# A hybrid decoder step on one core: normed rows held back behind the former pair's factors, two down groups in three token chunks, and the first problem's final rows ordered later

## The chip, the cores and the metric

The kernel runs on one core of a Trainium2 chip. The core has five engines that run on their own and meet through semaphores: TensorE (PE, with its weight loads shown as PEld), VectorE (DVE), ScalarE (ACT), GpSimd (POOL) and SyncE (SP), which here issues nearly all DMAs. The metric is the device time of one launch in microseconds (us). Times of this kernel's runs lie within 1 us of each other.

## The reference

One layer of a decoder for 1024 prompt tokens and 64 sample tokens (8 sequences of 8), 1088 tokens in all, with a model width of 1024:

```python
x += merge_out(attention(h), short_conv(h)) @ w_out          # h = rmsnorm(x) @ w_in, split in 11 parts
h = rmsnorm(x, norm_ffn);  gu = h @ w_gate_up                # 1024 -> 2 x 2816
x = x + (silu(gu[..., :D_FF]) * gu[..., D_FF:]) @ w_down     # 2816 -> 1024
gate = sigmoid(rmsnorm(x, norm_ple) @ w_ple_gate)            # 1024 -> 1024
x = x + (p @ w_ple) * gate                                   # 256 -> 1024
y = rmsnorm(x, norm_final)
```

The change touches the second half only: the norm before gate-up, the down projection, and the final norm's output. All of it is in float32 accuracy.

## The kernel before, in words

**Layout.** Activations are kept transposed: 128 features on the partitions, tokens along the free axis. `x1` holds the running sum as 8 blocks of 128 features by 1088 tokens. Every float32 operand is split into a high and a low part, and a product is three matmuls: high by high, low by high, high by low.

**Two problems.** From the output projection on, the tokens are cut into two problems of 544 (`p` = 0 and 1), and each into two halves of 272 columns (`CW`); a result fits one PSUM bank. There are five banks under the tag `pj` (for these results), two under `at` and one under `po`. The input projection, earlier, cuts the same 1088 tokens into three chunks instead, `CH`: 384, 384 and 320 columns.

**Order of the second half** (`order`, run by `run_rows` and `run_pair`): output projection of both problems; the rows of `w_ple` (`pw_pass`, both problems, copied out of PSUM by ACT in `evac_pw2`, and stored to DRAM); 22 gate-up blocks (`run_pair`, seven products instead of eight for a 2 by 2 block product; the first passes run as block 0 on problem 0, block 1 on problem 0, block 1 on problem 1, block 0 on problem 1); the down projection in four groups of the 22 blocks, `GR`: 4, 6, 6 and 6; then the gate of the last step (`w_ple_gate`) for problem 0 and, in two segments "a" (288 columns) and "b" (256), for problem 1.

**The planner.** The program is written out by a planner, `Weaver`. Every piece of work is a generator; it yields a condition (an event `Ev` with a planned time, or buffers of a ring). `Weaver` keeps a planned clock for each engine, and in each round steps the first side stream that is ready at PE's planned time (and while DVE and ACT are planned at most 5 us ahead of PE), otherwise the main stream of matmuls. What is stepped is written to the engines' instruction queues at once. So the planned times set only the order of instructions on each engine; on the chip an engine executes its queue in that order and waits where it must. `W.later(...)` orders a store or load when its planned time has come.

**The norm before gate-up.** When a problem's last block of `x1` is summed, `rstd` computes the factors and `norm` runs: it broadcasts them over the partitions by two matmuls into the `at` banks, and then, for each of four pairs of feature blocks (`b`, `b` + 4), takes three buffers of 128 by 544 from the ring `Q`, writes four normed half rows on DVE (L139) and spawns `factors`. That stream makes the seven combinations that the seven products need: three differences on DVE (L135), casts of two, two, two and one half rows to high parts on ACT (L131, `lead`), the remainders to low parts on DVE (L135, `rest`), one further difference, and gives its buffers back. `Q` has six buffers in the norm of problem 0 and ten in that of problem 1 (`places`, `room`). A row of `w_ple` needs two of them to begin.

**Down projection.** `down_pass` orders, for each of 8 output blocks `k`, the rows of a group: for each problem and each half one bank of 3 matmuls for each of the group's weight blocks. `evac_down` adds the bank to `x1` on DVE. `down_rows` reads the hidden rows back from DRAM by problem, and `row_in` splits them; `ev_md[g][p]` is the event that the rows of problem `p` are there.

**Final rows.** `fin` works through the token tiles of a segment (five for problem 0, three for "a", two for "b"): 8 transposes on PE (L197) into two banks (`at`, or `pj` for "b"), then `finish`: half a tile scaled on ACT (L131), half on DVE (L144), the banks given back, and the store ordered on SP (L163). For problem 0 and segment "a" `finish` runs after every tile, for "b" after both.

**Lines in the profile.** Helpers record most instructions, so rows carry their lines: L131 ACT, L135 and L139 and L144 DVE, L150 POOL, L154 and L190 and L197 and L186 PE, L163 the DMAs on SP.

Of the kernel before, what the change touches and what calls it, by code (L numbers as in the profile page):

```python
# [17 lines left out]
OP = mybir.AluOpType  # L18
# [8 lines left out]
KT = DM // P  # L27
# [14 lines left out]
CH = [(0, 384), (384, 384), (768, 320)]  # L42
LF = SEQ + 2

CW, PW = 272, 544
# [270 lines left out]
def hybrid_decoder_step(ctx, tc, I, O):  # L316
    nc = tc.nc
    W = Weaver(nc)
# [33 lines left out]
    def psum(tag):  # L352
        W.cur.t = max(W.cur.t, W.take(tag))
        return PS["pool"].tile([P, 512], F32, tag=tag, name=tag, bufs=PS["n"][tag])
# [266 lines left out]
    def free_ps():  # L621
        W.give("pj")
# [393 lines left out]
    g = {}  # L1016
# [604 lines left out]
    N_ = {}  # L1621
# [127 lines left out]
    def cols(ap):  # L1749
        return ap.rearrange("p a b -> p (a b)")  # L1750
# [6 lines left out]
    def room(p):  # L1757

        pool, a = (apool, "A") if p == 0 else (N_["bp"], "B")
        fac[p] = [pool.tile([P, 28, CW], F32, tag=f"{a}_{e}", name=f"f{p}_{e}") for e in ("hi", "lo")]  # L1760
        for e in ("hi", "lo"):
            t = pool.tile([P, 2, PW], F32, tag=f"{a}_{e}x", name=f"q{p}_{e}")
            extra.setdefault(p, []).extend([t[:, 0, :], t[:, 1, :]])
        places(*extra[p])

    def getq(n):
        out = []
        for _ in range(n):
            W.take("Q")
            out.append(Qs.popleft())  # L1770
        return out

    def giveq(*qs):
        for q in qs:
            if any(q is x for x in leaving):
                leaving[:] = [x for x in leaving if x is not q]
                if not leaving:
                    ev_left.t = W.cur.t
                continue
            Qs.append(q)  # L1780
            W.give("Q")
# [13 lines left out]
    def factor(p, i, b):  # L1795
        return [t[:, b * 7 + TI[i], :].bitcast(F32R) for t in fac[p]]

    def factors(p, b, qa, qb, qt, done):

        hi, lo = fac[p]  # L1800
        b11, b12, b21, b22, t1, t2 = (q[:, j * CW:(j + 1) * CW] for q in (qa, qb, qt) for j in range(2))

        def part(t, s, n):
            return cols(t[:, b * 7 + s:b * 7 + s + n, :])

        def lead(q, s, n):
            W.act(part(hi, s, n).bitcast(F32R), q, AF.Copy, n * CW)
            return W.cur.t

        def rest(q, s, n, t, pool):  # L1810
            W.cur.t = t
            (W.pool_tt if pool else W.tt)(part(lo, s, n).bitcast(F32R), q, part(hi, s, n), OP.subtract, n * CW)

        W.tt(t1, b12, b11, OP.subtract, CW)
        W.tt(t2, b22, t1, OP.subtract, CW)
        W.tt(b12, b22, b12, OP.subtract, CW)
        t0 = W.cur.t
        yield None
        tb = lead(qb, 2, 2)
        W.cur.t = t0  # L1820
        yield None
        ta, W.cur.t = lead(qa, 0, 2), t0
        tt = lead(qt, 4, 2)
        W.cur.t = tb
        yield None
        rest(qb, 2, 2, tb, False)
        W.tt(b21, b21, t2, OP.subtract, CW)
        yield None
        tc_ = lead(b21, 6, 1)
        W.cur.t = ta  # L1830
        yield None
        rest(qa, 0, 2, ta, False)
        giveq(qa)
        te, W.cur.t = W.cur.t, tt
        yield None
        rest(qt, 4, 2, tt, False)
        giveq(qt)
        te = max(te, W.cur.t)
        W.cur.t = tc_
        yield None  # L1840
        rest(b21, 6, 1, tc_, False)
        giveq(qb)
        W.cur.t = max(te, W.cur.t)
        done()
# [62 lines left out]
    def norm(p, gfun, ev):  # L1907

        x1 = N_["x1"]
        ns, ev_r = rs.pop(p)  # L1910
        yield ev_r
        if p not in fac:
            room(p)
        yield {"at": 2, "Q": 1}
        (dg,), bc = getq(1), [psum("at"), psum("at")]
        for j, (o, m) in enumerate(TT[p]):
            W.ts(dg[:, o:o + m], ident[:, :m], ns[:, 8 + j:9 + j], None, OP.mult, None, m)
        W.cur.t += 1.5
        yield None
        for h in range(2):  # L1920
            W.mm(bc[h][:, :CW], ones, dg[:, h * CW:(h + 1) * CW], CW, True, True, f32=True)
        giveq(dg)
        left, t0 = [4], W.cur.t

        def done():
            left[0] -= 1
            if left[0] == 0:
                ev.t = W.cur.t - 1.0
        for b in range(4):
            W.cur.t = t0  # L1930
            yield {"Q": 3}
            qa, qb, qt = getq(3)
            for q, k in ((qa, b), (qb, b + 4)):
                for h in range(2):
                    s = slice(h * CW, (h + 1) * CW)
                    W.stt(q[:, s], bc[h][:, :CW], gfun(k), x1[:, k, p * PW + h * CW:p * PW + (h + 1) * CW], OP.mult, OP.mult, CW)
            if b == 3:
                W.give("at", 2)
            W.spawn(factors(p, b, qa, qb, qt, done))

    def norm_rows(p, gfun, ev):

# [40 lines left out]
    def add_square(p, k, n, gfun, evs, last=False, how=None):  # L1983

        n[p] = n.get(p, 0) + 1
        s = square(p, k, n[p] == 1, last)
        if n[p] < KT:
            yield from s
            return
        n[p] = 0  # L1990
        yield from s
        start_rstd(p, 0.0 if p == "b" else 1.0 if gfun is g_ffn else 4.0)
        if gfun is None:
            return
        W.spawn((how or norm)(p, gfun, evs[p]))
# [56 lines left out]
    GR = [(0, 4), (4, 6), (10, 6), (16, 6)]  # L2052
    ev_near = Ev()
    ev_gu, ev_gr = [Ev(), Ev()], [Ev() for _ in GR]
    ev_md = [[Ev(), Ev()] for _ in GR]
    M = {}
# [32 lines left out]
            ev.t = W.cur.t  # L2089

    def evac_down(g, k, p, h, ps):
        xs = N_["x1"][:, k, p * PW + h * CW:p * PW + (h + 1) * CW]
        W.tt(xs, ps[:, :CW], xs, OP.add, CW)
        free_ps()
        if g == len(GR) - 1 and h == 1:
            W.spawn(add_square(p, k, n_down, g_ple, ev_h3, how=norm_rows))

    PLE_H = {0: {0: (0, CW), 1: (CW, CW)}, 1: {"a": SEG["a"], "b": SEG["b"]}}
    pw = {}

# [14 lines left out]
    def evac_ple(k, p, h, ps):  # L2115
        o, n = PLE_H[p][h]
        seg = 0 if p == 0 else h
# [36 lines left out]
    y_s = O["y_sample"].rearrange("b t d -> (b t) d")  # L2154
# [5 lines left out]
    def fin(p):  # L2160
        x1, c0 = N_["x1"], SEG[p][0]
        done = []
        if p == "a":
            y_places()
        yt = N_["bp"].tile([P, 5, DM], F32, tag="B_hi", name="y") if p == 0 else N_["y_ab"][p]

        def finish():
            ns, ev_r = rs[p]
            yield ev_r
            t1 = W.cur.t  # L2170
            for j, (o, m), tag, bk, t_ in done:
                W.cur.t = max(t1, t_)
                yield None
                y = yt[:m, j, :]
                r, tok = ns[:m, 8 + j:9 + j], c0 + o
                t2 = W.cur.t
                W.act(y[:, 0:512], bk[0][:m, :], AF.Copy, 512, scale=r)
                t3, W.cur.t = W.cur.t, t2
                W.ts(y[:, 512:], bk[1][:m, :], r, None, OP.mult, None, 512, fast=False)
                W.cur.t = max(t3, W.cur.t)  # L2180
                W.give(tag, 2)

                def store(tok=tok, m=m, y=y):
                    mp_ = max(0, min(m, SEQ - tok))
                    if mp_:
                        W.store(y_p[tok:tok + mp_], y[:mp_])
                    if mp_ < m:
                        W.store(y_s, y[mp_:])
                W.later(store)
            done.clear()  # L2190
        for j, (o, m) in enumerate(TT[p]):
            tag = "pj" if p == "b" else "at"
            yield {tag: 2}
            bk = [psum(tag), psum(tag)]
            for k in range(KT):
                yield ev_x[p][k]
                W.tr(bk[k // 4][:m, (k % 4) * P:(k % 4 + 1) * P], x1[:, k, c0 + o:c0 + o + m], ident)
            done.append((j, (o, m), tag, bk, W.cur.t))
            if p != "b" or j == 1:
                yield from finish()  # L2200
# [61 lines left out]
    def rows_of(src, k, evac, **kw):  # L2262
        return dict(block(src, k * P, evac, None, **kw), k=k)

    order = []
# [17 lines left out]
    def down_pass(g, ks, ps):  # L2283
        f0, n = GR[g]
        bs = [rows_of(I["w_down"], k, lambda *a: evac_down(g, *a), row0=f0 * P, nk=n) for k in ks]
        order.append(("rows", bs, ps, lambda: M[g], ev_md[g], 0, ev_gr[g] if ks[-1] == KT - 1 else None))

    def ple_pass(p):
        for ks in [(k,) for k in range(KT)] if p == 0 else [(0,), (1,), (2,), (3,), (4,), (5, 6, 7)]:
            order.append(("rows", [rows_of(I["w_ple_gate"], k, evac_ple) for k in ks], (p,), lambda: N_["h3"], ev_h3, 2, None, None,  # L2290
                          PLE_H))

# [183 lines left out]
```

## Time and profile before

| | |
|---|---|
| time, median of 3 runs | 1997.98 us (1997.33 to 1998.3) |
| profiled execution | 1997.44 us, span 1995.7 us |
| PE busy | 1944.2 us (97%) |
| DVE busy | 1277.0 us (64%) |
| POOL busy | 742.7 us (37%) |
| ACT busy | 713.1 us (36%) |
| mean granted PE clock | 0.989 |

Times in a trace count from the span's start. A group or timeline row names the line, the engine, the operation, output and inputs by the program's names (buffer numbers left out), the shapes, and in brackets the idle time of the engine before it and what ended it. A row of PE's waits gives the total, the number and the longest. A row of busy times by window gives the window, its length, busy time (and instructions) of PE, PEld, DVE, ACT and POOL, the granted PE clock as a share of full speed, the share of DMA engines busy, and GB/s. Matmuls are pipelined: the length shown of one is longer than the distance to the next one's start.

### The profile page before, as it was taken

The numbers are of one execution on the slowest core, as the hardware profiler recorded it, in microseconds if no ns is written. First come the engines' busy times: TensorE is split into PE (matmuls) and PEld (weight loads), VectorE is DVE, ScalarE is ACT, GpSimd is POOL, SyncE is SP. The second block draws the span as 40 slices with busy tenths as digits, with TensorE's granted clock in tenths as the row PEclk, the third lists the DMA queues.
The fourth block names the chain that finished last, engine by engine and source line by source line (L and its number), as shares of the span: only waits on it lengthen the run. The fifth ranks groups of instructions, "written<-read, shape, count | busy, mean of one in ns | idle before, by whom it ended". The sixth has DMA issues, their size and how long they took to land.

```text
span 1995.7 us, 36382 instructions
## 1 busy us (share of the span) xinstructions
PE 1944.2 (97%) x13585; PEld 1864.6 (93%) x13585; DVE 1277.0 (64%) x2727; ACT 713.1 (36%) x1448; POOL 742.7 (37%) x661
## 2 busy tenths in 40 slices
PE   8998999999999999999999899999999999999998
PEld 6987879999999999779999899999999999999988
DVE  6635899899988896323438776566666653314754
ACT  5354443312433325433334532232232322213543
POOL 2533445323223242214444233232232354424873
PEclk9999999999999999999999899999999999999999
DMA  4664325222222222446453332222222343212343
GB/s 151 177 192 110 107 83 151 65 56 73 78 73 55 56 64 72 125 118 187 127 157 113 131 95 86 66 81 81 71 79 79 122 151 106 91 43 85 105 152 96
DMA packets 291243, 205.27 MB, mean 103 GB/s; under 512 B 28448, under 2 KB 270680, under 8 KB 291066
## 3 DMA queue, kind: packets, MB, share of 16 engines
q1 hardware_dynamic: 290822, 202.85, 34.1%
q8 instruction: 107, 1.75, 0.4%
q14 instruction: 70, 0.57, 0.1%
q10 hardware_dynamic: 244, 0.09, 0.0%
HBM read 151.43 MB, written 51.31 MB: 102 GB/s over the span
## 4 chain that ended last, share of the span: by engine, by line
PE 81%; DVE 5%; POOL 2%; issue 2%; DMA 1%; ACT 1%; DVEq 0%; SPq 0%; POOLq 0%; ACTq 0%
PE pj L154 42%; PE pj L190 27%; PE at L186 5%; PE po L186 4%; PE pt L197 3%; POOL wl L150 1%; DVE scores L139 1%; DVE ru L135 0%; DMA q_hi<-ple_scr 0%; POOL x L150 0%; DVE junk L1225 0%; DVE x L135 0%; POOL whl L150 0%; DVE q_lo L135 0%; PE at L197 0%
## 5 line engine op out<-in xcount | busy, mean ns | idle before, releaser
L150 POOL TENSOR_TENSOR wl<-wraw,wh 128x512 fp32r<-128x512 f32 (+2 forms) x233 | 298.9, 1286 | 651.1 <-ACT wh L131 642.1
L190 PE MATMUL pj<-h_hi,wh 128*128 128x384 f32 (+2 forms) x1197 | 406.6, 340 | 0.3 <-ACT wh L131 0.3
L190 PE MATMUL pj<-h_hi,wl 128*128 128x384 f32 (+2 forms) x1197 | 393.6, 329 | 0.7 <-POOL wl L150 0.7
L190 PE MATMUL pj<-h_lo,wh 128*128 128x384 f32 (+2 forms) x1197 | 393.3, 329 | 0.0
L131 ACT ACTIVATE wh<-wraw 128x512 fp32r<-128x512 f32 (+2 forms) x233 | 141.5, 610 | 279.7 <-PE pj L154 137.6
L190 PEld LDWEIGHTS pj<-h_hi,wh 128*128 128x128 f32 (+1 forms) x1197 | 225.9, 189 | 16.3 <-issue 12.4
L190 PEld LDWEIGHTS pj<-h_lo,wh 128*128 128x128 f32 (+1 forms) x1197 | 226.1, 189 | 2.5
L190 PEld LDWEIGHTS pj<-h_hi,wl 128*128 128x128 f32 (+1 forms) x1197 | 225.4, 188 | 1.8 <-POOL wl L150 1.1
L154 PE MATMUL pj<-f_hi,whl 128*128 128x272 f32 x1056 | 206.0, 288 | 0.0
L154 PE MATMUL pj<-f_hi,wl 128*128 128x272 f32 x704 | 203.6, 289 | 0.5 <-DVE wl L135 0.5
L154 PE MATMUL pj<-f_hi,wh 128*128 128x272 f32 x704 | 203.3, 289 | 0.0
L154 PE MATMUL pj<-f_lo,wh 128*128 128x272 f32 x704 | 202.6, 288 | 0.0
L154 PE MATMUL pj<-m_hi,wh 128*128 128x272 f32 x644 | 186.2, 289 | 1.0 <-ACT tha L131 0.5
L154 PE MATMUL pj<-m_hi,wl 128*128 128x272 f32 x644 | 185.9, 289 | 0.0
L154 PE MATMUL pj<-m_lo,wh 128*128 128x272 f32 x644 | 185.8, 289 | 0.0
L135 DVE TENSOR_TENSOR x<-pj,x 128x272 f32<-128x272 f32 x160 | 69.5, 437 | 173.6 <-PE pj L154 170.5
L154 PEld LDWEIGHTS pj<-f_hi,whl 128*128 128x128 f32 x1056 | 168.8, 189 | 0.0
L154 PE MATMUL pj<-f_lo,whl 128*128 128x272 f32 x528 | 152.4, 289 | 0.0
L154 PEld LDWEIGHTS pj<-f_hi,wl 128*128 128x128 f32 x704 | 132.9, 189 | 0.7 <-DVE wl L135 0.7
L154 PEld LDWEIGHTS pj<-f_hi,wh 128*128 128x128 f32 x704 | 132.8, 189 | 0.0
L154 PEld LDWEIGHTS pj<-f_lo,wh 128*128 128x128 f32 x704 | 132.7, 189 | 0.0
L154 PEld LDWEIGHTS pj<-m_hi,wh 128*128 128x128 f32 x644 | 121.4, 188 | 1.5 <-ACT tha L131 0.8
(364 smaller groups left out, 4566.9 us busy)
## 6 DMA issues: line engine op xcount, KB each, us to landing
wraw<-in_w_in SPq DMA_DIRECT2D x112, 256.0 KB
wraw<-in_w_gate_up SPq DMA_DIRECT2D x92, 256.0 KB
wraw<-in_w_down SPq DMA_DIRECT2D x40, 256.0 KB
wraw<-in_w_out SPq DMA_DIRECT2D x32, 256.0 KB
wraw<-in_w_ple_gate SPq DMA_DIRECT2D x32, 256.0 KB
x<-in_x_prompt SPq DMA_DIRECT2D x13, 512.0 KB
m_scr<-q_hi SPq DMA_DIRECT2D x18, 272.0 KB
q_lo<-m_scr SPq DMA_DIRECT2D x18, 272.0 KB
```

What stands on the lines that cost most here:

```text
L131: self.nc.scalar.activation(out, in_, func, **kw)
L135: self.nc.vector.tensor_tensor(out, a, b, op=op)
L139: self.nc.vector.scalar_tensor_tensor(out, a, s, b, op0=op0, op1=op1)
L150: self.nc.gpsimd.tensor_tensor(out, a, b, op=op)
L154: self.nc.tensor.matmul(ps, l, r, start=start, stop=stop)
L186: self.nc.tensor.matmul(ps, l, r, start=start, stop=stop)
L190: self.nc.tensor.matmul(ps, l, r, start=start, stop=stop)
L197: self.nc.tensor.transpose(ps, in_, ident)
```

## The change

Three edits, and one store moved.

1. `norm` yields, ahead of the rows of pair `b` > 0, the event `begun[b - 1]`. `factors` sets it (with planned time 0) once it has ordered its three differences and the casts of `qb`, `qa` and `qt`.
2. Groups 1 and 2 of the down projection run over three token chunks, `c0`, `c1`, `c2` (the columns of `CH`), in place of two problems of two halves. The first chunk waits for problem 0's rows, the two others for problem 1's. `evac_down` adds a chunk of that width. Groups 0 and 3 stay as they were.
3. In `finish`, 4.0 us are added to the planned time for problem 0, each time that it runs, ahead of the scaling.
4. The store of the sample rows of `y` is issued by ACT (`nc.scalar.dma_start`) in place of SP.

```diff
-    def factors(p, b, qa, qb, qt, done):
+    def factors(p, b, qa, qb, qt, begun, done):
...
         ta, W.cur.t = lead(qa, 0, 2), t0
         tt = lead(qt, 4, 2)
+        begun.t = 0.0
         W.cur.t = tb
         yield None
...
+        begun = [Ev() for _ in range(4)]
         for b in range(4):
             W.cur.t = t0
+            if b > 0:
+                yield begun[b - 1]
             yield {"Q": 3}
...
-            W.spawn(factors(p, b, qa, qb, qt, done))
+            W.spawn(factors(p, b, qa, qb, qt, begun[b], done))
...
     def evac_down(g, k, p, h, ps):
-        xs = N_["x1"][:, k, p * PW + h * CW:p * PW + (h + 1) * CW]
-        W.tt(xs, ps[:, :CW], xs, OP.add, CW)
+        c0, n = DOWN_H[p][h] if p in DOWN_H else (p * PW + h * CW, CW)
+        xs = N_["x1"][:, k, c0:c0 + n]
+        W.tt(xs, ps[:, :n], xs, OP.add, n)
...
+    DOWN_H = {f"c{c}": {c // 2: CH[c]} for c in range(3)}
...
             yield ev_r
+            W.cur.t += 4.0 if p == 0 else 0.0
             t1 = W.cur.t
...
                     if mp_ < m:
-                        W.store(y_s, y[mp_:])
+                        nc.scalar.dma_start(y_s, y[mp_:])
...
-        order.append(("rows", bs, ps, lambda: M[g], ev_md[g], 0, ev_gr[g] if ks[-1] == KT - 1 else None))
+        evs, halves = ev_md[g], None
+        if 0 < g < len(GR) - 1:
+            ps, halves, evs = tuple(DOWN_H), DOWN_H, dict(zip(DOWN_H, (evs[0], evs[1], evs[1])))
+        order.append(("rows", bs, ps, lambda: M[g], evs, 0, ev_gr[g] if ks[-1] == KT - 1 else None, None, halves))
```

## The prediction

> **What bounds the kernel now.** I read the page's busy table, the chain by engine, PE's waits, and then busy time stage by stage.
>
> ```profile
> PE 1944.2 (97%) x13585; PEld 1864.6 (93%) x13585; DVE 1277.0 (64%) x2727; ACT 713.1 (36%) x1448; POOL 742.7 (37%) x661
> PE 81%; DVE 5%; POOL 2%; issue 2%; DMA 1%; ACT 1%; DVEq 0%; SPq 0%; POOLq 0%; ACTq 0%
> ```
>
> PE is busy for 97% of the span and carries 81% of the chain, so the end moves only where PE idles, where its clock falls, or where its matmuls get cheaper. The profiled execution took 1997.44 us (span 1995.7); the sum is made against that. The runs' median, 1997.98, is 0.5 above it. PE's waits, from 990 to 1160 us and then from 1880 to the end:
>
> ```profile
> PE pj L154 <- ACT q L131: 8.0, 1, 8.0
> PE pj L154 <- DVE wl L135: 0.5, 1, 0.5
> PE pj L154 <- ACT q_hi L131: 0.3, 1, 0.3
> ...
> PE at L197 <- DVE y L144: 2.7, 1, 2.7
> PE at L197 <- ACT y L131: 0.7, 1, 0.7
> ```
>
> The 8.0 us lies in the w_ple rows. The timeline there (start, length, engine):
>
> ```profile
> 1109.07 0.40 ACT L131 ACTIVATE q_lo<-pj 128x272 f32<-128x272 f32 x1 [0.30 <-PE pj L154]
> 1109.60 0.97 DVE L139 SCALAR_TENSOR_TENSOR q<-at,gvec,x 128x272 f32<-128x272 f32 x2 [3.40 <-PE at L186]
> 1114.57 0.43 DVE L135 TENSOR_TENSOR q_hi<-q 128x272 f32<-128x272 f32 x1
> 1115.86 0.66 ACT L131 ACTIVATE f_hi<-q 128x544 fp32r<-128x544 f32 x1 [3.78 <-DVE q L135]
> 1121.21 0.40 ACT L131 ACTIVATE q<-pj 128x272 f32<-128x272 f32 x1 [0.56 <-DVE f_lo L135]
> 1121.66 0.59 PE L154 MATMUL pj<-pT_hi,wh 128*128 128x272 f32 x1 [7.97 <-ACT q L131]
> ```
>
> DVE first makes the normed rows of three pairs (1109.60 to 1114.57), and only then the differences of the first pair that ACT's second cast (1115.86) needs. ACT copied a bank out at 1109.07 and the next at 1121.21; between them stand only casts. PE fills its five pj banks and stops. The order is the planner's: three pairs hold nine of the ten q tiles, and a w_ple row asks for two, so its copies are planned after the casts. Busy time (PE, PEld, DVE, ACT, POOL, clock) after the norm's broadcast: rest of w_ple, first gate-up pass, second gate-up pass (both on the first problem); then the cold stretch; then down groups 1 and 2; then the wait of 2.7 us near the end.
>
> ```profile
> 1109.60:1135.20 25.60, 17.28 (x117) 16.70 (x116) 22.85 (x49) 14.22 (x34) 1.53 (x1) 0.80 0.33 117
> 1135.20:1145.70 10.50, 10.50 (x86) 10.50 (x85) 9.07 (x13) 5.04 (x13) 4.68 (x3) 1.00 0.42 138
> 1145.70:1156.70 11.00, 10.53 (x84) 10.31 (x83) 8.44 (x17) 4.86 (x8) 4.28 (x3) 1.00 0.39 121
> ...
> 1121.66:1127.28 5.62, 5.27 (x22) 4.95 (x22) 5.55 (x11) 2.63 (x9) 0.00 (x0) 0.50 0.27 99
> ...
> 1649.30:1721.70 72.40, 72.40 (x580) 72.40 (x579) 22.76 (x39) 15.35 (x29) 26.81 (x22) 1.00 0.31 99
> 1721.70:1794.10 72.40, 72.40 (x580) 72.40 (x579) 22.80 (x39) 15.13 (x29) 27.19 (x23) 1.00 0.18 53
> ...
> 1935.20:1938.04 2.84, 0.11 (x1) 0.00 (x0) 2.41 (x10) 1.59 (x4) 0.57 (x2) 1.00 0.46 144
> ```
>
> Rows that part 1 uses: the first problem's norm, the dense stretch of 272-column matmuls (start, length, count), and the end of the second problem's norm.
>
> ```profile
> 1065.33 0.64 ACT L131 ACTIVATE f_hi<-q_hi 128x544 fp32r<-128x544 f32 x1
> ...
> 1067.38 0.90 DVE L139 SCALAR_TENSOR_TENSOR q_hi<-at,gvec,x 128x272 f32<-128x272 f32 x2
> ...
> 1612.76 223.21 PE pj L154 x1776
> ...
> 1145.33 0.43 DVE L135 TENSOR_TENSOR f_lo<-q_hi,f_hi 128x272 fp32r<-128x272 f32 x1
> ```
>
> **Part 1, rows held back.** No instruction is added or removed; what moves is the order on DVE and ACT, and with it the SP stores behind those copies. With the hold, pair 1's four row products are ordered only after pair 0's three differences and three casts, so six or fewer tiles are taken at first and the w_ple rows find their two: their ACT copies are ordered between the casts. In the norm of the first problem nothing should move: its second pair (1067.38) already comes after the first one's casts.
>
> What is there to win: a 272-column matmul costs 223.21 / 1776 = 125.7 ns when dense. The stretch from 1109.60 to 1156.70 lasts 47.1 us and holds 117 + 86 + 84 = 287 PE matmuls, 36.1 us. So 11.0 us are loss: waits of 8.0, 0.3 and 0.5, and about 2.5 of cold clock (5.62 us for 22 matmuls that need 2.8, less the 0.3). What is late next is DVE: the third gate-up pass, at 1156.70, needs all four pairs of the second problem, and by then DVE has done 22.85 + 9.07 + 8.44 = 40.4 us of work: 4.3 more than PE's 36.1. Some of it (the last banks' additions) may come later, about 1 us by a 0.43 us row each; some new DVE wait on ACT comes on top. I take 3.7 us of new stall, in pieces, and a **gain of 7.3**. Bounds: 11.0 if all of DVE's surplus can be put off, 0 if DVE keeps its old pace to 1156.70. A loss I exclude: DVE does the same work, starts it no later, and was 11 us early (last f_lo of the norm at 1145.33).
>
> On the clock the rows say: after the 8.0 us wait it stood at 0.50 for 5.6 us and cost 2.5; around the 2.7 us wait near 1938 it stayed at 1.00. So a new stall costs more if it comes in one long piece; that case is in rival A. The Trainium skill (TensorE: Matmul & The Clock Gate, "Why this matters for your kernels") asks for no PE gap beyond about 3 us; both rows agree. By that rule the 3.7 us in one piece would be past the limit, and the gain would be an estimated 5.
>
> **Part 2, three chunks.** Groups 1 and 2 have 8 output rows each with 6 weight blocks times 3 products. Each row was 4 banks of 18 matmuls over 272 columns; now it is 3 banks of 18 over 384, 384 and 320. Those widths run in the input projection; a run of each (first and last row shown; 22 and 24 starts apart), and the last split of group 2's rows:
>
> ```profile
> 955.54 0.34 PE L190 MATMUL pj<-h_lo,wh 128*128 128x384 f32 x1
> ...
> 959.36 0.33 PE L190 MATMUL pj<-h_hix,wl 128*128 128x384 f32 x1
> 959.54 0.31 PE L190 MATMUL pj<-h_hi,wh 128*128 128x320 f32 x1
> ...
> 963.05 0.34 PE L190 MATMUL pj<-h_hi,wh 128*128 128x384 f32 x1
> ...
> 1660.16 1.83 POOL L150 TENSOR_TENSOR m_lo<-q_lo,m_hi 128x544 fp32r<-128x544 f32 x1
> ```
>
> 384 columns: 3.82 / 22 = 173.6 ns. 320: 3.51 / 24 = 146.3 ns. A row: 72 x 125.7 = 9.05 us before, 18 x (173.6 + 173.6 + 146.3) = 8.88 after, 0.17 less; 16 rows give **2.7 us**. Both stages have PE busy for 72.40 of 72.40 us, so all of it counts. DVE's additions fall from 64 to 48 and it is busy for 23 of 72 us. The second chunk now needs the second problem's rows some 3 us earlier in a group; the last of group 2's were split by 1662, 60 us ahead of 1721.70.
>
> Bounds: 2.7, and 0 if a new wait of PE on a bank or a weight block, of which the stages have none now, eats it. The Trainium skill (TensorE: Matmul & The Clock Gate, "Back-to-back issue gap") gives a warm gap of columns / 2.4 plus 2.5 ns, so a fixed part of 2.5 per matmul, not the 12 that these rows imply; by it 288 matmuls fewer would bring only 0.7 us. The measured rows decide.
>
> **Part 3, final rows.** The added 4.0 is planning time; it stands before every one of the first problem's five tiles. Their scalings on ACT and DVE, the next tile's transposes (they need the two at banks back) and the SP store are each ordered later.
>
> ```profile
> 1937.16 0.69 ACT L131 ACTIVATE y<-at,ns 128x512 f32<-128x512 f32 x1 [1.13 <-DVE ns L1898]
> 1938.04 1.09 PE L197 MATMUL at<-ident,x 128*128 128x128 f32 x8 [2.74 <-DVE y L144]
> 1943.65 0.68 ACT L131 ACTIVATE y<-at,ns 32x512 f32<-32x512 f32 x1 [0.37 <-PE at L197]
> ...
> 1945.87 0.38 SPq L163 DMA_DIRECT2D q<-ple_scr  x1
> 1950.46 0.46 DVE L135 TENSOR_TENSOR q_hi<-q_hi,q 128x288 f32<-128x288 f32 x1 [3.21 <-DMA q<-ple_scr]
> 1961.90 2.55 DMA q<-ple_scr
> ```
>
> PE stood 2.7 us behind the second tile's transposes because the scaling waited for its factors; another 0.7 later. Gate matmuls of the second problem fill both, 3.4 us. Against that: the tiles, 1.6 us apart (1937.16 to 1943.65), now lie some 5.6 apart, so the last comes 20 us later, and their five stores mix with loads of w_ple rows that are on the chain. A load behind stores landed after 4.6 us (1945.87 to 1950.46), one without after 2.55: 2.0 each. From 1951 the chain runs through POOL, DVE and those loads, so not all of PE's lead arrives. I take **1.5 us of gain**, bounds 3.4 gain to 2.6 loss (three such loads, 6.0, less the 3.4).
>
> The last store moves from SP to ACT's queue. Nothing is queued behind it there: it is ACT's last work.
>
> ```profile
> 1989.99 1.19 SPq L163 DMA_DIRECT2D out_y_prompt<-y_ab  x2
> 1991.23 0.59 SPq L163 DMA_DIRECT2D out_y_sample<-y_ab  x1
> ...
> 1.17 0.59 ACTq L662 DMA_DIRECT2D gtmp<-in_norm_mix  x1
> ```
>
> An ACT issue takes 0.59 us too, but starts beside SP's last: **0.6 gained**, bounds 0.7 to 0.
>
> **Sum.** 1997.44 - 7.3 - 2.7 - 1.5 - 0.6 = 1985.3 us.
>
> **Rivals.** DVE's longest wait for ACT's casts in the second problem's norm:
>
> ```profile
> 1134.18 0.73 DVE L135 TENSOR_TENSOR f_lo<-q_hi,f_hi 128x544 fp32r<-128x544 f32 x1 [2.44 <-ACT f_hi L131]
> ```
>
> (A) DVE takes the bound at once: it keeps its 40.4 us and this wait. Then 42.8 of the 47.1 us stay: 1997.44 - 4.3 - 4.8 = 1988.3, and with a cold stretch like the old one (2.5) 1990.8. For it: DVE's surplus over PE; against: additions can trail PE by a few banks, and that wait belongs to the old order. I put it at 1990.5, since a stall that long comes in one piece.
>
> (B) The hold does not do what it says: the norm stands ahead of w_ple in the planner and takes the tiles anyhow. Then only parts 2 and 3 count: 1997.44 - 4.8 = 1992.6. Against it: each pair now needs casts that are ordered only as PE's planned time passes.
>
> (C) Slower: the first problem's tiles hold the two at banks beyond the moment when the second problem's first segment wants them for its transposes:
>
> ```profile
> 1975.78 0.33 PE at L197
> ```
>
> That moment comes 10.0 us earlier with parts 1 and 2, at 1965.8. The last tile is done at about 1937.2 - 10.0 + 4 + 4 x spacing, 1953.6 with 5.6 us. The mechanism decides from a spacing of 8.7, and must eat the 10.6 us of parts 1, 2 and the store and 4 more to make the kernel slower: a spacing of 12.4. At 13 it would be 1983.2, 17.4 late: 1997.44 - 10.6 + 17.4 = 2004.2. For it: the delay repeats for each tile; against: 13 is over twice the 5.6.
>
> **How the numbers follow.** A measurement tells 0.2%, 4.0 us, from no change: below 1994.0 is faster, above 2002.0 slower. Forecast 0.60 (all faster); better than 1980 (every part at its bound gives 1980.0) 0.05; A 0.20 (0.16 faster, 0.04 within); B 0.10 (0.05, 0.05); C 0.05 (0.01 within, 0.04 slower). Faster 0.86, same 0.10, slower 0.04. The range 1980 to 1993 holds the forecast, A and over half of B; the forecast alone would be 1980 to 1990.
>
> **What would show it.** Right: no PE wait on an ACT copy above 1 us in the w_ple rows, clock 1.00 there, four row products followed by differences on DVE; new small PE waits on DVE before the third gate-up pass; groups 1 and 2 in about 71.1 us each with 384- and 320-column rows; no PE wait of 2.7 us on y. Wrong: a wait over 4 us at the third pass (A), the old wait still there (B), PE or SP waiting on late y tiles near the end (C).

## The result, and the profile after

The changed kernel takes 1986.47 us in the median of its runs (1985.4 to 1988.04), the kernel before 1997.95 (1997.33 to 1998.3). The ratio is 0.9942, 95% interval 0.9928 to 0.9955; a second measurement, below, gave 0.9939 (0.9923 to 0.9955). The forecast was 1985.3, so the sum came out nearly right. Three of its four terms did not, as the rows show.

The profiled execution took 1988.04 us (span 1986.2). The page of the changed kernel, busy table and chain by engine:

```profile
PE 1942.3 (98%) x13297; PEld 1863.8 (94%) x13297; DVE 1272.9 (64%) x2711; ACT 713.1 (36%) x1448; POOL 744.3 (37%) x661
PE 82%; DVE 4%; POOL 2%; issue 2%; DMA 1%; ACT 1%; SPq 0%; DVEq 0%; POOLq 0%; ACTq 0%
```

288 matmuls are gone, and PE still carries the chain. PE's waits of the changed kernel from 990 to 1160 us:

```profile
PE pj L154 <- DVE whl L135: 2.6, 1, 2.6
PE pj L154 <- DVE wl L135: 0.5, 1, 0.5
```

The 8.0 us on an ACT copy have gone, and 2.6 us on the low part of a weight tile (`whl`) are new. How the order on the engines changed, in the changed kernel's timeline (DVE, then ACT):

```profile
1111.07 0.90 DVE L139 SCALAR_TENSOR_TENSOR q_hi<-at,gvec,x 128x272 f32<-128x272 f32 x2
...
1113.21 0.43 DVE L135 TENSOR_TENSOR q_hi<-q 128x272 f32<-128x272 f32 x1
...
1115.84 0.40 ACT L131 ACTIVATE q_lo<-pj 128x272 f32<-128x272 f32 x1 [0.36 <-PE pj L154]
1116.13 0.65 ACT L131 ACTIVATE f_hi<-q_hi 128x544 fp32r<-128x544 f32 x1
...
1117.77 0.39 ACT L131 ACTIVATE q_lo<-pj 128x272 f32<-128x272 f32 x1
```

Four row products (two rows of two, from 1110.18), then the differences of the first pair; and ACT copies banks out between the casts. Busy time by window in the changed kernel (the end of the `w_ple` rows; the 6 us behind the new wait; and the stretch from the norm's broadcast to the point 443.4 us ahead of group 0's first matmul, which is where the stretch 1109.60 to 1156.70 of before ended):

```profile
1110.20:1125.30 15.10, 15.10 (x122) 15.06 (x121) 14.43 (x31) 11.38 (x29) 1.62 (x1) 1.00 0.55 193
1136.00:1142.00 6.00, 5.99 (x26) 5.99 (x27) 5.96 (x11) 3.71 (x7) 1.29 (x1) 0.50 0.47 134
1110.18:1151.86 41.68, 38.53 (x282) 38.06 (x281) 40.06 (x75) 24.11 (x52) 10.15 (x7) 0.92 0.41 132
```

In the `w_ple` rows PE no longer waits and the clock stays at 1.00. The whole stretch lasts 41.7 us, 47.1 before, and of these **DVE works 40.1** (the third busy time). Behind the new wait the clock stood at 0.50 for 6 us: 26 matmuls that need 26 x 0.1257 = 3.3.

The landmark that divides part 1 from the rest is the first matmul of down group 0, in the timeline of before:

```profile
1600.09 0.29 PE L154 MATMUL pj<-m_hi,wh 128*128 128x272 f32 x1
```

and in that of the changed kernel:

```profile
1595.25 0.28 PE L154 MATMUL pj<-m_hi,wh 128*128 128x272 f32 x1
...
1979.61 1.41 DVE L144 TENSOR_SCALAR y_ab<-pj,ns 128x512 f32<-128x512 f32 x2
```

From the broadcast to this matmul it was 490.5 us (1600.09 - 1109.60) and is 485.1: 5.4 less. From there to the end of the last scaling on DVE it was 390.5 (the scaling began at 1989.16 and took 1.41) and is 385.8: 4.7 less, for parts 2 and 3 together. From that scaling to the end of the span it was 5.1 and is 5.2. How far such distances can be trusted: in the profiles of four kernels that leave part 1 out (the one before, `e_store`, `e_chunk` and `e_final` below) the first is 490.2 to 490.5 us, and in four that leave out parts 2 and 3 (the one before, `e_store`, `e_hold` and `e_q5`) the second is 390.0 to 391.7. The broadcast itself came 0.6 later, by work far ahead of the change. That is 9.5 in all between the two profiled spans; the medians differ by 11.5.

### The profile page after: what moved, and what is told of

It is laid out like the page before. It is cut to its first block, busy times and chain, and to the rows that moved or that the text cites. A ratio compares the mean times of both kernels' runs of the same rounds, so it can differ in the third digit from the quotient of the medians.

```text
span 1986.2 us, 35764 instructions
## 1 busy us (share of the span) xinstructions
PE 1942.3 (98%) x13297; PEld 1863.8 (94%) x13297; DVE 1272.9 (64%) x2711; ACT 713.1 (36%) x1448; POOL 744.3 (37%) x661
## 4 chain that ended last, share of the span: by engine, by line
PE 82%; DVE 4%; POOL 2%; issue 2%; DMA 1%; ACT 1%; SPq 0%; DVEq 0%; POOLq 0%; ACTq 0%
PE pj L154 44%; PE pj L190 27%; PE at L186 5%; PE po L186 4%; PE pt L197 3%; DVE scores L139 0%; DVE ru L135 0%; PE at L197 0%; POOL wl L150 0%; DVE junk L1225 0%; POOL rt L150 0%; POOL x L150 0%; DVE x L135 0%; DMA wraw<-in_w_down 0%; POOL x L2154 0%
## 5 line engine op out<-in xcount | busy, mean ns | idle before, releaser
L135 DVE TENSOR_TENSOR x<-pj,x 128x272 f32<-128x272 f32 (+2 forms) x144 | 67.0, 468 | 173.8 <-PE pj L154 170.6
L154 PE MATMUL pj<-m_hi,wh 128*128 128x272 f32 (+2 forms) x586 | 176.0, 300 | 0.9 <-ACT tha L131 0.5
L154 PE MATMUL pj<-m_hi,wl 128*128 128x272 f32 (+2 forms) x586 | 175.6, 300 | 0.0
L154 PE MATMUL pj<-m_lo,wh 128*128 128x272 f32 (+2 forms) x586 | 175.6, 300 | 0.0
L150 POOL TENSOR_TENSOR whl<-wraw,whl 128x512 fp32r<-128x512 f32 (+1 forms) x67 | 91.9, 1374 | 78.9 <-ACT whl L131 78.6
```

The lines of the kernel that those rows point to most:

```text
L135: self.nc.vector.tensor_tensor(out, a, b, op=op)
L150: self.nc.gpsimd.tensor_tensor(out, a, b, op=op)
L154: self.nc.tensor.matmul(ps, l, r, start=start, stop=stop)
```

## The experiments

Each kernel is the one before, or the changed one, with one edit. They were timed on several occasions, on which the kernel before took 1997.7 to 2001.5 us in the median; so kernels are compared by their ratios to it. The theory to be tested: the hold frees `q` tiles, so that ACT's copies are ordered between casts; what is left of that loss is DVE's; the chunks bring what the spacings say; the 4.0 bring about 2; the store brings nothing. The rivals are those of the prediction.

**Part 1 alone** (`e_hold`): the three lines with `begun` put into the kernel before.

> The kernel before with part 1 alone (the hold). The prediction's theory: the waits of 8.8 us in the w_ple rows and the cold stretch go, some 3 us of waits on DVE come back, so 5 to 8 us faster than before (ratio 0.9960 to 0.9975): 5.4 if the 2.6 us wait on a low part of a weight (near 1136 us in the changed kernel) is followed by 6 us at half clock as it was there, near 8 in executions where it is not. Rival A (DVE keeps its old pace): 4 to 4.8 less what a cold stretch costs, and one DVE wait of over 4 us. Rival B (the hold does nothing): within 0.5 us of before.

Measured: 1991.67 us against 1997.68, ratio 0.9972 (0.9961 to 0.9983), 6.0 us. PE's waits from 1000 to 1165 us in the kernel with the hold alone:

```profile
PE pj L154 <- DVE whl L135: 2.6, 1, 2.6
PE pj L154 <- DVE wl L135: 2.3, 2, 1.8
```

and its stretch from the broadcast on, by windows as above:

```profile
1112.69:1153.86 41.17, 36.24 (x282) 35.40 (x281) 40.29 (x75) 24.11 (x52) 10.26 (x7) 1.00 0.41 133
```

Here the 2.6 us wait was not followed by a cold clock (1.00 throughout), but another wait of 1.8 us came behind it, and the stretch is 41.2 us long, not 39. DVE works 40.3 of the 41.2. So without the cold stretch the gain is 5.9 us and not 8: the length goes with DVE's busy time and not with the clock. That is what rival A expects, in pieces and without the 2.4 us wait on ACT that it added.

**Two tiles kept free instead of the hold** (`e_q5`):

```diff
-            yield {"Q": 3}
+            yield {"Q": 5 if p == 1 and b > 0 else 3}
             qa, qb, qt = getq(3)
```

> The kernel before, no hold; instead each pair of the second problem's norm after the first one asks for five free q tiles and takes three, so that two stay for a w_ple row. No instruction is added. If the shortage of q tiles made the 8.0 us wait, it goes here too, and the time comes near that of the hold alone (5 to 8 us faster). If what counts is that the former pair's casts are ordered first, whatever is free, the wait stays and the time is within 1 us of before.

Measured: 1992.64 us, ratio 0.9976 (0.9966 to 0.9986), 5.0 us. Its timeline has two pairs' row products in one go (four rows of L139 together at 1113.57, where the changed kernel has two and then the differences), and copies on ACT ahead of the casts all the same:

```profile
1113.57 1.72 DVE L139 SCALAR_TENSOR_TENSOR q_hi<-at,gvec,x 128x272 f32<-128x272 f32 x4
...
1118.88 0.70 ACT L131 ACTIVATE q_lo<-pj 128x272 f32<-128x272 f32 x2
1119.44 0.69 ACT L131 ACTIVATE f_hi<-q_hi 128x544 fp32r<-128x544 f32 x1
```

Its stretch from the broadcast on, by windows:

```profile
1112.68:1154.19 41.51, 37.60 (x282) 36.68 (x281) 40.02 (x74) 23.86 (x52) 10.68 (x7) 0.96 0.40 132
```

The 8.0 us wait is gone here too, and DVE is busy for 40.0 of 41.5 us. It was the shortage of `q` tiles that made it; the order of rows and casts is only one way to keep two tiles free.

**Part 2 alone** (`e_chunk`): `evac_down`, `DOWN_H` and `down_pass` as in the change.

> The kernel before with part 2 alone (three chunks in down groups 1 and 2). By the measured spacings (384 columns 173.6 ns, 320 columns 146.3, 272 columns 125.7): 2.7 us faster, the two stages 72.4 us each before and 71.1 after, with PE busy throughout. By a fixed part of 2.5 ns a matmul: 0.7 us faster, 72.1 each. If a new wait eats it: 0, with a wait of PE on a bank or weight block between 1649 and 1795 us.

Measured: 1994.92 us, ratio 0.9985 (0.9975 to 0.9995), 2.8 us with an interval from 1.0 to 5.0. DVE's additions in this kernel, where an output row has three banks of 384, 384 and 320 columns; shown is the same bank of two rows that follow each other:

```profile
1692.58 0.56 DVE L135 TENSOR_TENSOR x<-pj,x 128x384 f32<-128x384 f32 x1 [2.56 <-PE pj L154]
...
1701.48 0.56 DVE L135 TENSOR_TENSOR x<-pj,x 128x384 f32<-128x384 f32 x1 [2.56 <-PE pj L154]
```

and in the kernel before, with four banks of 272:

```profile
1692.18 0.44 DVE L135 TENSOR_TENSOR x<-pj,x 128x272 f32<-128x272 f32 x1 [1.84 <-PE pj L154]
...
1701.21 0.44 DVE L135 TENSOR_TENSOR x<-pj,x 128x272 f32<-128x272 f32 x1 [1.83 <-PE pj L154]
```

8.90 us a row against 9.03: 0.13 each, 2.1 for 16 rows. From group 0's first matmul (1601.66) to the end of the last scaling (1989.73) it is 388.1 us, 2.4 less than before. So a gain of 2.1 to 2.8. The 0.7 of a fixed 2.5 ns would be 0.04 a row; the rows' 0.13 rules it out.

**Part 3 alone** (`e_final`): the line with 4.0.

> The kernel before with the 4.0 us of planning time before each tile of the first problem's final rows alone. Theory: PE's waits on y (2.7 and 0.7) go and 1.5 to 3.4 us reach the end. The comparison of the two profiles gave 1.9 between the start of group 3 and the end. If stores among the loads of w_ple rows eat it: 0 to 2.6 slower, with a wait on those loads before 1965 us.

Measured: 1995.5 us, ratio 0.9990 (0.9979 to 1.0001), 2.2 us; the interval just reaches no change. In its profile the distance from group 0's first matmul (1600.41) to the end of the last scaling (1988.06) is 387.7 us, 2.8 less than before. PE's wait on `y` from 1880 us on, in this kernel:

```profile
PE at L197 <- DVE y L144: 1.0, 1, 1.0
```

and in its timeline the ACT rows of the first problem's tiles, the first and the last of five:

```profile
1938.63 0.69 ACT L131 ACTIVATE y<-at,ns 128x512 f32<-128x512 f32 x1 [0.63 <-DVE ns L1898]
...
1963.81 0.66 ACT L131 ACTIVATE y<-at,ns 32x512 f32<-32x512 f32 x1
```

Of 3.4 us of waits on `y`, 1.0 is left. The tiles stand 6.3 us apart (25.18 / 4), where 5.6 was predicted, and the end of the last scaling is not held up by them.

**The store alone** (`e_store`): the line with `nc.scalar.dma_start`. Of this kernel there is one execution.

> The kernel before with the last store alone moved from SP to ACT's queue. The prediction's term: from the end of the last scaling on DVE to the end of the span 4.5 us in place of 5.1, since its issue of 0.59 us runs beside SP's last. Rival: the time to land, not the issue, ends the span, and it stays 5.0 to 5.2.

Its timeline (the span ends at 1999.2):

```profile
1992.64 1.41 DVE L144 TENSOR_SCALAR y_ab<-pj,ns 128x512 f32<-128x512 f32 x2
1994.14 0.55 ACTq L2188 DMA_DIRECT2D out_y_sample<-y_ab  x1
```

From the end of the scaling (1994.05) to the end it is 5.15 us, as before (5.1). Issued 0.6 earlier, the store ends the span no earlier: the term was 0. The DMA engines' share of busy time tells why; it is the last figure but one, for 3.3 us from 0.25 us behind that scaling on, first in the kernel before, then in this one:

```profile
1990.80:1994.10 3.30, 0.00 (x0) 0.00 (x0) 0.00 (x0) 0.00 (x0) 0.00 (x0) 0.50 0.99 315
...
1994.30:1997.60 3.30, 0.00 (x0) 0.00 (x0) 0.00 (x0) 0.00 (x0) 0.00 (x0) 0.76 0.99 315
```

Both kernels keep the 16 DMA engines 99% busy at 315 GB/s, so an earlier issue finds no free engine: the bytes of the stores, and not the moment of the last issue, set this time.

**The changed kernel again** (`e_after`).

> The changed kernel again, with more executions. The single parts measured 6.0 (hold), 2.8 (chunks) and 2.2 us (final rows); if they add up and the store on the ACT queue brings nothing, 11.0 us faster than before, 1986.5. If the store brings its 0.6: 11.6. If the parts get in each other's way (the hold's lead eaten near the end): 8 or less.

Measured: 1986.84 us against 1999.12, ratio 0.9939 (0.9923 to 0.9955), 12.3 us. The parts alone add up to 6.0 + 2.8 + 2.2 = 11.0, well inside the interval (8.9 to 15.4): they do not get in each other's way. This profile, of the same program, has no cold stretch behind the 2.6 us wait. PE's waits from 1000 to 1165 us:

```profile
PE pj L154 <- DVE whl L135: 2.6, 1, 2.6
PE pj L154 <- DVE wl L135: 2.4, 2, 1.8
```

The whole stretch, by windows:

```profile
1110.49:1151.70 41.21, 36.23 (x282) 35.39 (x281) 40.29 (x75) 24.10 (x52) 10.24 (x7) 1.00 0.41 133
```

In its place stands the wait of 1.8. PE lost 2.7 to the clock in one execution and 1.9 more to waits in the other, and the stretch is 41.7 or 41.2 us long; DVE is busy for 40 of it both times.

**One low part moved to POOL** (`e_pool`):

```diff
-                (W.tt if kind in (6, 5, 4) else W.pool_tt)(...)
+                (W.tt if kind in (6, 5, 4) and not (kind == 4 and it["pair"]["no"] < 1) else W.pool_tt)(...)
```

> The changed kernel, with the low part of the fourth-kind weight tile (r22) of the first gate-up pair on POOL instead of DVE: one row of 0.68 us leaves DVE, one of 1.3 to 1.5 us goes to POOL, which stands nearly idle. If the 2.6 us wait near 1136 us is only a matter of that row's place behind the last pair's differences, it goes, with the cold stretch where there is one: 2.6 to 5.4 us faster than the changed kernel. If DVE's whole work in the stretch is the bound, the wait comes back at the next low part that DVE makes (there were 1.8 us on such a one in the run of the hold alone): 0.7 us faster at most, and 0 if DVE rows with two operands in SBUF take longer beside POOL rows, as the differences at 1132.04 and 1133.27 (1.19 and 1.39 us, not 0.43) seem to.

Measured: 1987.73 us, ratio 0.9942 (0.9927 to 0.9956), so no gain over the changed kernel; from the broadcast to group 0's first matmul its profile has 487.8 us, against 484.6 in the second profile of the changed kernel. PE's longest wait from 1000 to 1165 us in this kernel:

```profile
PE pj L154 <- DVE wl L135: 4.9, 2, 4.3
```

its stretch from the broadcast on, by windows:

```profile
1111.12:1155.54 44.42, 38.17 (x282) 37.32 (x281) 41.81 (x75) 24.10 (x52) 11.85 (x8) 0.92 0.38 123
```

and in its timeline one DVE row beside two POOL rows:

```profile
1129.17 3.00 POOL L150 TENSOR_TENSOR whl<-wraw,whl 128x512 fp32r<-128x512 f32 x2 [6.00 <-ACT whl L131]
1130.94 1.77 DVE L135 TENSOR_TENSOR wsum<-wraw,wsum 128x512 f32<-128x512 f32 x1
```

The wait on `whl` went and came back as 4.3 us on the next low part that DVE makes. A row of 0.68 us left DVE, yet its busy time rose from 40.3 to 41.8; among its rows the sum at 1130.94 took 1.77 us in place of 0.68 while POOL worked.

**Two POOL rows moved to DVE** (`e_lock`), the opposite:

```diff
-                (W.tt if kind in (6, 5, 4) else W.pool_tt)(...)
+                (W.tt if kind in (6, 5, 4) or kind in (1, 3) and (kind, it["pair"]["no"]) in ((3, 0), (1, 1)) else W.pool_tt)(...)
```

> The changed kernel with the two POOL rows that stand beside the last pair's differences (low part of the first gate-up pair's third-kind tile, and of the second pair's first-kind tile; 1131.75 and 1133.25 in the changed kernel's second profile, 1.53 and 1.46 us) made by DVE. If DVE rows with two operands in SBUF stand blocked until a POOL row ends, the two differences take 0.43 us each in place of 1.20 and 1.39, the low part for which PE waits comes 1.7 us sooner and that wait falls from 2.6 to about 0.9 us; DVE's whole work changes by 2 x 0.68 - 1.7 = -0.3 us, so the time by no more than 1 us. If POOL has nothing to do with it, the differences keep 1.2 and 1.4 us and the kernel is 1 to 2 us slower.

Measured: 1988.34 us against 2001.47, ratio 0.9937 (0.9923 to 0.9951), the changed kernel's within 0.5 us. The second profile of the changed kernel has these rows in question, in its timeline:

```profile
1131.75 1.53 POOL L150 TENSOR_TENSOR whl<-wsum,whl 128x512 fp32r<-128x512 f32 x1 [1.90 <-ACT whl L131]
1132.39 1.20 DVE L135 TENSOR_TENSOR q<-q_lo 128x272 f32<-128x272 f32 x1
1133.25 1.46 POOL L150 TENSOR_TENSOR wl<-wraw,wh 128x512 fp32r<-128x512 f32 x1
1133.62 1.39 DVE L135 TENSOR_TENSOR q<-q_lo,q 128x272 f32<-128x272 f32 x1
```

and the kernel with those POOL rows on DVE:

```profile
1133.34 0.43 DVE L135 TENSOR_TENSOR q<-q_lo 128x272 f32<-128x272 f32 x1
1133.80 0.45 DVE L135 TENSOR_TENSOR q<-q_lo,q 128x272 f32<-128x272 f32 x1
```

PE's waits on `whl` in it (total, times, longest):

```profile
PE pj L154 <- DVE whl L135: 1.1, 2, 0.9
```

and its stretch by windows:

```profile
1111.48:1152.68 41.20, 37.87 (x282) 36.96 (x281) 39.56 (x77) 24.15 (x52) 6.89 (x5) 0.96 0.41 133
```

The two differences take 0.43 and 0.45 us when no POOL row runs beside them, and PE's wait on `whl` falls from 2.6 to 0.9, as foretold. In the changed kernel each of them ended 0.3 us after a POOL row did (1133.28, then 1134.71): it was blocked until then. The Trainium skill (SBUF — State Buffer, "Who interferes with whom") says that a DVE instruction with two SBUF inputs contends with a GpSimd instruction that reads SBUF, and that the one issued second fully blocks; the rows agree. The stretch stays at 41.2 us, though: two rows more on DVE, and a clock of 0.96 in this execution.

**DVE relieved of 5.8 us** (`e_cut`):

```diff
-        rest(qa, 0, 2, ta, False)
+        rest(qa, 0, 2, ta, p == 1)
...
-        rest(qt, 4, 2, tt, False)
+        rest(qt, 4, 2, tt, p == 1)
```

with `rest` making a plain ACT copy where its last argument is true.

> The changed kernel with a part of the computation changed: of the second problem's four pairs in that norm, the low parts of qa and of the two differences qt (8 DVE rows of 0.72 us) are made by ACT as plain copies, so these low parts hold the whole value and not the rest that the high part leaves. DVE loses 5.8 us of the 46 that it works between 1110 and 1160, ACT gains 5.3 us. If DVE's whole work is the bound there, PE's waits on DVE in the first two gate-up passes (2.6, 1.8, 0.5, or less of them and a cold stretch) fall to 1.5 us or less, and the kernel is 3 to 5 us faster than the changed one. If the waits come from the place of single rows, they stay, and the time is within 1 us.

Measured: 1988.82 us, ratio 0.9939 (0.9923 to 0.9954): no gain. The stretch of this kernel by windows; then one of DVE's waits in it, and a piece of the chain that ended last there:

```profile
1116.13:1157.03 40.90, 37.73 (x282) 36.97 (x281) 34.23 (x66) 27.36 (x59) 9.81 (x7) 0.96 0.41 134
```

```profile
DVE q L135 <- ACT q L131: 2.3, 1, 2.3
...
1131.68 1.25 ACT f_lo L131 x2
```

DVE works 34.2 us now and stands idle 6.7, but the stretch is only 0.3 shorter than in the changed kernel's second profile. PE waits 2.5 us for the same low part as before: on DVE's queue it stands behind the last pair's products, these behind a bank addition, and that waited 2.3 us for an ACT copy. So the gain expected if DVE's whole work were the bound did not come: with 6 us of DVE's load gone, the order of the queues makes a stretch of nearly the same length. Two of the copies that ACT got stand in the chain ahead of that wait (1.25 us at 1131.68), so the run does not tell what less work on DVE would give with no more on ACT.

**A third gate-up pass on the first problem first** (`e_third`):

```diff
-    for fs_, ps_ in (((0,), (0,)), ((1,), (0, 1)), ((0,), (1,)), (range(2, NF), (0, 1))):
+    for fs_, ps_ in (((0,), (0,)), ((1,), (0,)), ((2,), (0, 1)), ((0,), (1,)), ((1,), (1,)), (range(3, NF), (0, 1))):
```

> The changed kernel with a third gate-up pass on the first problem ahead of the first one on the second problem (passes 0, 1, 2 on the first; then 2, 0, 1 on the second, so pairs 0 and 1 are both loaded and prepared a second time, as pair 0 was already). If the rest of the loss is DVE's surplus that falls due at the first pass on the second problem, the longer cover takes 2 to 4 us more. If DVE's rows for the second problem stand ahead of the weights' low parts whatever comes later, the waits of 2.6 and 1.8 us in the first two passes stay, and the time is within 1.5 us of the changed kernel.

Measured: 1995.99 us, ratio 0.9975 (0.9962 to 0.9989): about 7 us slower than the changed kernel, which neither expectation held; the 2.6 us wait on `whl` is still there. PE's longest group of waits from 1000 to 1165 us in it:

```profile
PE pj L154 <- DVE wl L135: 6.8, 3, 4.5
```

and its stretch by windows:

```profile
1112.46:1160.28 47.82, 38.46 (x298) 37.43 (x296) 46.92 (x81) 27.80 (x59) 15.22 (x10) 0.97 0.40 129
```

From the broadcast to group 0's first matmul (1603.67) it is 491.2 us, 6.6 more than the 484.6 (1595.09 - 1110.49) of the changed kernel's second profile; DVE's busy time in the stretch (its end set back from that matmul by the same 443.4 us) is 46.92 - 40.29 = 6.6 more. The weights prepared once more are work in the one place where DVE is full, and the kernel got longer by as much as DVE's busy time did. ACT and POOL got work there too (27.8 and 15.2 us busy, 24.1 and 10.2 before), so that DVE's share alone did it is not shown.

**Low parts ahead of the last pair** (`e_early54`):

```diff
-            if kind == 0:
+            if kind == 0 or kind in (5, 4) and it["pair"]["no"] < 2:
                 low()
```

> The changed kernel with the low parts of the fourth- and fifth-kind tiles of the first two gate-up pairs ordered right behind their casts in place of at a later planned time. No instruction is added or removed; on DVE these lows now stand ahead of the last pair's differences of the second problem's norm. If the waits come from the place of single rows on DVE's queue, the 2.6 and the 1.8 us go, nothing of the kind comes back, and the kernel is 3 to 5 us faster than the changed one. If DVE has more work there than PE, the waits come back later (on another low part, or on a factor at the first pass on the second problem), and the time is within 1 us.

Measured: 1990.32 us, ratio 0.9957 (0.9942 to 0.9972): about 3 us slower than the changed kernel by the ratios, whose intervals overlap, and 3.6 by the two profiles from the broadcast to group 0 (1593.80 - 1105.64 = 488.2, against 484.6). PE's longest wait in it:

```profile
PE pj L154 <- DVE wl L135: 6.8, 1, 6.8
```

and the window around it:

```profile
1130.00:1140.00 10.00, 2.91 (x22) 2.50 (x20) 9.35 (x17) 3.12 (x6) 2.85 (x2) 0.85 0.26 77
```

Both old waits are gone and one of 6.8 us on a later low part has come, while DVE is busy 9.35 of 10 us. It is the second outcome that was written down, but dearer.

**The dose of part 3** (`e_8`): 8.0 in place of 4.0.

> The changed kernel with 8.0 us of planning time before each tile of the first problem's final rows in place of 4.0. The waits on y are gone already, so nothing is left to win. By the working of rival C (tiles now 6.2 us apart, then about 10.2; the last must be done before the second problem's first segment wants its banks, and this fails from a spacing of 8.7): 6 to 10 us slower than the changed kernel, with PE waiting on late y tiles near the end. If the planner orders gate matmuls and the end's chain around the tiles: within 1 us of it.

Measured: 1988.03 us, ratio 0.9943 (0.9925 to 0.9960), against 1986.84 and 0.9939 for 4.0: no difference that these runs tell. In its timeline, the first and the last of the first problem's tiles on ACT, and the very last scaling there:

```profile
1937.87 0.67 ACT L131 ACTIVATE y<-at,ns 128x512 f32<-128x512 f32 x1
...
1975.92 0.66 ACT L131 ACTIVATE y<-at,ns 32x512 f32<-32x512 f32 x1
...
1982.29 1.23 ACT L131 ACTIVATE y_ab<-pj,ns 128x512 f32<-128x512 f32 x2
```

The tiles are 9.5 us apart (38.05 / 4), beyond the 8.7 from which rival C was to decide. But the very last scaling on ACT comes 868.9 us after the broadcast (at 1113.38 here), just as in the changed kernel's second profile (1979.36 - 1110.49 = 868.9), and the last one on DVE ends 0.5 us later: the tiles behind follow more closely.

None of these kernels beats the changed one.

## Why the prediction was right, and where it was wrong

**Part 1, forecast 7.3, measured 5.4 to 6.0.** The mechanism stood: the copies are ordered between the casts, the 8.0 us wait and its cold stretch go, and rival B fell; `e_q5` shows the tile shortage as the cause. The step that failed is the 3.7 us of new stall, and in it the guess that "about 1 us" of DVE's surplus could come later. Nothing was put off: 74 or 75 DVE rows lie in the stretch and 76 before, and it is 41.2 to 41.7 us long with 40.0 to 40.3 of DVE's busy time in it, in four profiles (changed kernel twice, hold alone, two tiles kept). Against the prediction's 36.1 us of PE work the new loss is 5.1 to 5.6 us. (The 287 matmuls behind the 36.1 count some twice that straddle two windows; one window over the stretch has 282, 35.4 us. And all bounds together give 1979.6, not 1980.0. Neither moves the forecast.) The words "in pieces" were right for the second profile of the changed kernel and for the hold alone; in the first a piece of 2.6 us was followed by 6 us at half clock, although the 2.7 us wait of before had not been.

So the measured length is what **rival A's mechanism** gives without the 2.4 us of a wait on ACT's casts that it added: 40.4 + 0.8 of DVE idle, not 42.8. The forecast would have come closer with DVE's 40.4 of before as the floor. That the number is the same after is in part chance, since busy time is not all work: in the changed kernel's second profile five rows that overlap POOL rows (at 1129.41, 1132.39, 1133.62 and 1146.17, and the second of two from 1142.18) took 4.1 us longer than such rows take alone (0.43 and 0.68), and four in the kernel before 3.1.

That DVE's amount of work is the whole story is not shown, either. More work there made the kernel longer by as much (`e_third`), and rows moved about do not help (`e_pool`, `e_lock`, `e_early54`); but less of it (`e_cut`) did not help, with more of it on ACT and the order unchanged. Whether an order exists that wins back the other 5 us is open; three reorderings did not find it.

**Part 2, forecast 2.7, measured 2.1 by the rows, 2.4 by the profile, 2.8 by the times.** Right; the rows of the input projection overstated a row's gain by 0.04 us (8.88 forecast, 8.90 measured, and 9.03 in place of 9.05 before). The gap that the Trainium skill (TensorE: Matmul & The Clock Gate, "Back-to-back issue gap") gives, columns / 2.4 plus 2.5 ns, is there for a matmul by itself and not, as here, for a stream with a weight load to each; by it a row would be an estimated 0.04 shorter, and 0.13 was measured.

**Part 3, forecast 1.5, measured 2.2 to 2.8.** With the 4.0 alone 1.0 us of the waits on `y` is left; in the changed kernel none is, but there PE also comes to these tiles late, behind some 3 us at half clock (below), which cost it an estimated 1.6. Too much was taken off for the loads and the chain at the end: the step that failed is "from 1951 the chain runs through POOL, DVE and those loads, so not all of PE's lead arrives". In the changed kernel no such wait is left there, and PE carries the chain through it, as the longest piece of its chain from 1920 to 1990 us shows:

```profile
1951.80 13.90 PE pj L154 x108
```

Rival C fell with `e_8`: beyond the spacing where it was to decide the end came at most 0.5 us later, because the second problem's tiles have slack among themselves.

**The store, forecast 0.6, measured 0.** An issue that starts earlier is not a store that lands earlier when the DMA engines are full (99% busy in both kernels); the interval from the last scaling to the end was 5.1 to 5.2 us from either queue.

The errors are 1.3 to 1.9 too much for part 1, 0.6 for the store and 0.3 or so for part 2, and 0.7 to 1.3 too little for part 3. By the profiles the forecast gain of 12.1 was 1 to 2 us too high; that the median came within 1.2 us of it, with a spread of single runs of several us, is partly luck.

## What to carry to other kernels

When a stall on one engine is removed, take the next engine's busy time in that same stretch as a first estimate of the new length, all of it, unless a row shows work that the consumer does not need yet. Taking work off that engine need not shorten the stretch (`e_cut`), since its queue's order can hold the same length. A stall of a planned order can come from a shortage of buffers; then any way to keep some free will do. Moving an elementwise row from DVE to GpSimd did not relieve DVE here, where DVE's own rows read two SBUF operands at that time.

## What the runs showed of the hardware that was not expected

**DVE rows blocked by POOL rows.** A 272-column difference took 1.20 and 1.39 us beside a POOL row and 0.43 without; a 512-column sum 1.77 and 0.68. A row with one operand in PSUM was not slowed (0.43 at 1132.04 in the changed kernel's second profile, inside the POOL row at 1131.75).

**The clock's fall differs between executions.** The same 2.6 us wait at the same instruction was followed by 6 us at 0.50 in one execution of the changed kernel and by 1.00 in the other. Near the end the clock fell in both, behind 18 one-column matmuls that took 1.94 us and a wait of 0.43 ahead of them (by windows, first profile):

```profile
1923.90:1927.00 3.10, 3.10 (x15) 3.10 (x14) 0.80 (x1) 1.23 (x3) 2.94 (x3) 0.50 0.37 103
```

The same one-column matmuls were followed by such a fall in 11 of the 14 traces; in the one of the kernel before, and in those of `e_final` and `e_store`, the clock kept 1.00. The prediction had no term for it. The Trainium skill (TensorE: Matmul & The Clock Gate, "What's actually happening") tells of a free-running activity window of 3413 ns, which could explain why the clock falls in one execution only; but the 2.6 us here are shorter than the idle window that it names, and than the 3 us that the prediction took as the limit. What decides is not shown. Over 35 executions of the kernel before, the time goes with the mean granted clock: 2001.8 us in the mean of the 4 at 0.988, 1994.6 in the mean of the 3 at 0.992. Single runs of it differ by up to 10 us, not by the 1 us of its first three, and differences of 1 us are not told apart here.
